# A hybrid attention and mLSTM encoder: 368 weight reloads moved from SP's DMA queue to POOL's

## The chip, the core and the metric

The kernel runs on one core of one Trainium2 chip. A core has a matrix engine (PE, whose weight loads are listed apart as PEld), a vector engine (DVE), a scalar engine (ACT), a general engine (POOL) and SP, which here only issues DMAs. All DMAs are carried out by the same 16 DMA engines. The metric is the device time of one execution in microseconds (us). The kernel before takes 2937.11 us, the median of three runs (2936.93 to 2938.26).

## The reference, cut to what matters

Two sequences (1024 and 2048 tokens of 1024 features, plus 16 learned meta tokens) go through one encoder layer with shared weights:

```python
def _encoder_layer(h, g_pre, w_in, b_in, na_rpb, ml_conv_w, ml_head_g, w_a, w_b, w_out, g_post):
    xn = _rmsnorm(h, g_pre)
    proj = xn @ w_in + b_in                    # 1024 -> 6672 columns
    na_q, na_k, na_v, na_z, ml_qk, ml_v, ml_z, ml_o, ml_g, mg = jnp.split(proj, SPLIT_IDX, axis=-1)
    ya = _neighbourhood_attention(na_q, na_k, na_v, na_rpb)     # 8 x 16 windows on a grid 64 wide
    ya = (ya * jax.nn.silu(na_z)) @ w_a
    yb = (_mlstm_branch(ml_qk, ml_v, ml_g, ml_o, ml_conv_w, ml_head_g) * jax.nn.silu(ml_z)) @ w_b
    ga, gb = jnp.split(jax.nn.sigmoid(mg), 2, axis=-1)
    y = (ga * ya + gb * yb) @ w_out
    return h + _rmsnorm(y, g_post)
```

Everything is 32-bit floating point.

## The kernel before, in words

**Products in two parts.** A 32-bit operand is split into a high part and a rest (`hi`, `lo`), and each product is three matmuls: high by high, high by low, low by high. So every weight tile exists twice, as `whi` and `wlo`, each 128 partitions by up to 1056 words, mostly 512 KB.

**Two streams, one hand-written order on PE.** `run` interleaves a dense stream (the projections and the last products, in the order of `PLAN`) with a sparse stream (`STEPS`: the mLSTM of sequence 0, the attention of sequence 0, the same two for sequence 1). Each generator yields its cost, and the two are advanced in step. PE's order is exactly the order in which the program is written. The order on the other engines and in the DMA queues is set when the program is built, by a scheduler that works from its own estimate of when each instruction could run; within an engine or a queue the order is then fixed, and an instruction that waits holds those behind it.

**Dense stages.** A projection stage (`group`) takes four weight tiles and runs them over two halves of 512 tokens: 24 matmuls a tile and half (`fm_half`, through `mm3`, lines 144 to 146). `tm_unit` (lines 412 to 414) does the columns that are wanted with tokens on the partitions, 24 matmuls of 256 columns for each 128 tokens. A last stage (`final`) for 512 tokens is eight steps of 24 matmuls through `mm3`, one weight pair each, with two gate tiles `tg` read from DRAM per step (line 1267), and then four steps of 4 x 24 matmuls of 256 columns (`prods`, lines 1304 to 1306), two weight pairs each. There are six last stages, and 15 entries in the plan.

**Where the weights come from.** `requests` lists every weight tile in the order of its use. `wload` (line 215) loads a tile from the inputs into `wraw` when it is asked for the first time. `wpump` then makes `whi` (ACT, line 233) and `wlo` (DVE or POOL, line 236) and writes both to DRAM (line 240). When the same tile is asked for again, `wpump` reads the two parts back, lines 230 and 231: two DMAs. There are 184 such reloads, 368 DMAs. `whi` and `wlo` have four buffers each (`NBW`); `wdone`, called when the last matmul on a tile has been written down, frees one and calls `wpump`, so that a reload stands in its queue directly behind the matmuls that free its buffer and waits for them there.

**Queues.** Almost every DMA of the kernel is issued by SP, 2352 of them with the reloads: stores of the projections, loads for the sparse stream, `tg`, the residual input, the output. SP's DMAs report on eight semaphores in turn, and a DMA waits until the one that used its semaphore before, eight places ahead in the queue, has landed. POOL issues 14 DMAs: the one-hot rows `qB` (line 561) and the masks `kx` (line 637) of the attention. Beside them POOL does 82 small memsets (`gt` lines 563 and 564, `g_t` lines 724 and 725, `raw` lines 840 and 842, `va` lines 876 and 877, `st` line 972, `ss` line 287), eight small copies and three of the subtractions of line 236.

**Loads of the sparse stream that the text speaks of:** `qr`, `kr` (`twice`, line 550) at the start of an attention head, `hn`, `tog`, `szg` (line 1170) in the mLSTM's last normalisation, `xh`, `xl` (line 317), the two parts of 512 tokens of the input read back.

Of the kernel before, what the change touches and what calls it, by code (L numbers as in the profile page):

```python
# [9 lines left out]
F32 = mybir.dt.float32  # L10
# [100 lines left out]
class K:  # L111
# [107 lines left out]
    def wpump(self):  # L219


        nc, wp = self.nc, self.wp
        self.wload()
        while self.wraw and self.wout < NBW:
            key, raw, nk, w = self.wraw.popleft()
            n = nk * w
            hi = wp.tile([P, 4 * WU], F32R, name="whi", bufs=NBW)
            lo = wp.tile([P, 4 * WU], F32R, name="wlo", bufs=NBW)
            if raw is None:
                for x, d in zip((hi, lo), self.wkept[key]):  # L230
                    nc.sync.dma_start(x[:, :n].bitcast(F32), d[:, :])
            else:
                nc.scalar.activation(hi[:, :n], raw[:, :n], AF.Copy)
                self.nu += 1
                eng = nc.vector if self.nu > 4 else nc.gpsimd
                eng.tensor_tensor(lo[:, :n], raw[:, :n], hi[:, :n].bitcast(F32), op=ALU.subtract)
                self.wkept[key] = []
                for x, part in ((hi, "h"), (lo, "l")):
                    d = self.dp.tile([P, n], F32, name=f"w{part}{len(self.wkept)}")
                    nc.sync.dma_start(d[:, :], x[:, :n].bitcast(F32))  # L240
                    self.wkept[key].append(d)
            self.wrdy.append([x[:, :n].rearrange("p (k c) -> p k c", k=nk) for x in (hi, lo)])
            self.wout += 1
            self.wload()
# [1248 lines left out]
```

## Time and profile before

| what | us |
|---|---|
| median of three runs | 2937.11 |
| the profiled execution | 2935.2 |
| its span, first to last instruction | 2933.4 |
| PE idle at the start, waiting for `xr` (line 307) | 22.5 |
| PE idle on the other waits of the table of waits, together | 80.3 |
| SP waiting for PE at line 231, the three largest rows | 321.0 |

The span is what the engines' instructions cover; the profiled execution is 1.8 us longer. A row of the profile's table of waits names the instruction that waited, the one that released it, the total, the number of times and the longest. A stretch of the span is described by the busy time of each engine in it, the granted share of PE's clock, the share of time the 16 DMA engines were busy, and the rate in GB/s. In a timeline the columns are start, duration, engine, line, operation, what is written and read, and the number of instructions.

### The profile page before, as it was taken

How to read it: one execution, taken by the hardware profiler on the slowest of the kernel's cores; microseconds unless marked ns; L12 is line 12 of the kernel's file. 1: busy time of each engine (PE TensorE's matmuls, PEld its weight loads, DVE VectorE, ACT ScalarE, POOL GpSimd, SP SyncE). 2: the span in 40 equal slices, each digit the busy share in tenths (PEclk: the TensorE clock that was granted, in tenths of full speed). 3: DMA queues.
4: the chain of work that ended last, by engine and by line, in shares of the span. 5: the costliest groups of instructions: out<-in, count | busy, mean ns of one | idle time of the engine just before them, and what ended most of it. 6: DMA issues, size and time to landing. Idle time of an engine off the chain costs nothing.

```text
span 2933.4 us, 49345 instructions
## 1 busy us (share of the span) xinstructions
PE 2820.8 (96%) x17488; PEld 2510.8 (86%) x17488; DVE 1747.6 (60%) x4722; ACT 1288.7 (44%) x3114; POOL 23.1 (1%) x107
## 2 busy tenths in 40 slices
PE   6999999999799999999999999989999999989998
PEld 6998898899689988888887998977888888879797
DVE  5233566556556665465568776565555557777843
ACT  4213546433344444456566554413444445435421
POOL 1000000000000000000000000000000000000000
PEclk9999999999899999999999999999999999999999
DMA  9655667656775654568679898488568658897875
GB/s 350 219 179 181 197 218 256 232 182 207 255 232 153 198 175 134 168 232 298 197 234 363 277 313 290 136 263 272 172 196 283 191 174 272 245 280 236 283 273 194
DMA packets 438760, 675.25 MB, mean 230 GB/s; under 512 B 52240, under 2 KB 253024, under 8 KB 438512
## 3 DMA queue, kind: packets, MB, share of 16 engines
q1 hardware_dynamic: 437392, 669.41, 70.1%
q0 software_dynamic: 1120, 2.69, 0.4%
q8 instruction: 137, 2.24, 0.3%
q14 instruction: 111, 0.91, 0.1%
HBM read 455.05 MB, written 216.90 MB: 229 GB/s over the span
## 4 chain that ended last, share of the span: by engine, by line
PE 83%; DMA 9%; DVE 5%; ACT 1%; issue 1%; SPq 1%; DVEq 0%; ACTq 0%
PE pj L144 15%; PE pj L145 15%; PE pj L146 15%; PE pj L412 6%; PE pj L413 6%; PE pj L414 6%; PE sm L701 3%; PE pj L1304 3%; PE pj L1306 3%; PE pj L1305 3%; PE tr L689 2%; DMA tg<-gt 2%; PE sc L665 1%; PE sc L664 1%; PE sm L146 1%; PE sm L145 1%
## 5 line engine op out<-in xcount | busy, mean ns | idle before, releaser
L144 PE MATMUL pj<-xh,whi 128*128 128x512 f32 (+1 forms) x1824 | 722.2, 396 | 2.4 <-DVE xl L310 2.2
L145 PE MATMUL pj<-xl,whi 128*128 128x512 f32 (+1 forms) x1824 | 701.3, 384 | 0.6 <-DVE xl L310 0.6
L146 PE MATMUL pj<-xh,wlo 128*128 128x512 f32 (+1 forms) x1824 | 699.8, 384 | 0.0
L412 PE MATMUL pj<-whi,xh 128*128 128x256 f32 (+3 forms) x1576 | 450.8, 286 | 0.0
L413 PE MATMUL pj<-wlo,xh 128*128 128x256 f32 (+3 forms) x1576 | 444.7, 282 | 0.0
L414 PE MATMUL pj<-whi,xl 128*128 128x256 f32 (+3 forms) x1576 | 444.2, 282 | 0.0
L146 PEld LDWEIGHTS pj<-xh,wlo 128*128 128x128 f32 x1824 | 344.6, 189 | 72.3
L144 PEld LDWEIGHTS pj<-xh,whi 128*128 128x128 f32 x1824 | 345.2, 189 | 57.3 <-DVE xl L310 2.6
L145 PEld LDWEIGHTS pj<-xl,whi 128*128 128x128 f32 x1824 | 345.9, 190 | 53.3 <-DVE xl L310 0.8
L412 PEld LDWEIGHTS pj<-whi,xh 128*128 128x128 f32 (+1 forms) x1576 | 294.3, 187 | 1.2
L413 PEld LDWEIGHTS pj<-wlo,xh 128*128 128x128 f32 (+1 forms) x1576 | 294.0, 187 | 1.1
L414 PEld LDWEIGHTS pj<-whi,xl 128*128 128x128 f32 (+1 forms) x1576 | 294.1, 187 | 0.9
L692 DVE TENSOR_TENSOR pts<-tr,pts 96x512 fp32r<-96x512 f32 (+2 forms) x192 | 132.2, 688 | 159.4 <-ACT pts L691 158.3
L672 ACT ACTIVATE prb<-sc,mx 128x384 f32<-128x384 f32 (+2 forms) x192 | 119.4, 622 | 238.2 <-DVE mx L668 234.1
L1304 PE MATMUL pj<-whi,mh 128*128 128x256 f32 x768 | 221.0, 288 | 0.4 <-DMA whi<-wh 0.4
L1306 PE MATMUL pj<-whi,mlo 128*128 128x256 f32 x768 | 217.6, 283 | 2.1 <-DVE mlo L1287 2.1
L1305 PE MATMUL pj<-wlo,mh 128*128 128x256 f32 x768 | 217.2, 283 | 0.0
L691 ACT ACTIVATE pts<-tr 96x512 fp32r<-96x512 f32 (+2 forms) x192 | 114.3, 595 | 170.0 <-PE tr L689 169.3
L421 DVE TENSOR_TENSOR stT<-pj,bb 128x256 f32<-128x256 f32 (+3 forms) x197 | 83.1, 422 | 145.3 <-PE pj L414 141.2
L144 PE MATMUL pj<-yh,whi 128*128 128x512 f32 x384 | 158.0, 412 | 11.0 <-DVE tg L1283 11.0
L668 DVE CUSTOM_DVE_ANT_1 sc<-sc,gt 128x384 f32<-128x384 f32 (+2 forms) x192 | 118.9, 619 | 73.2 <-PE sc L665 67.4
L146 PE MATMUL pj<-yh,wlo 128*128 128x512 f32 x384 | 153.4, 399 | 0.0
(234 smaller groups left out, 5067.5 us busy)
## 6 DMA issues: line engine op xcount, KB each, us to landing
whi<-wh SPq DMA_DIRECT2D x176, 512.0 KB
wlo<-wl SPq DMA_DIRECT2D x176, 512.0 KB
wh<-whi SPq DMA_DIRECT2D x64, 512.0 KB
wl<-wlo SPq DMA_DIRECT2D x64, 512.0 KB
wraw<-w_in SPq DMA_DIRECT2D x48, 512.0 KB
gt<-st SPq DMA_DIRECT2D x96, 256.0 KB
tg<-gt SPq DMA_DIRECT2D x96, 256.0 KB
xh<-xh SPq DMA_DIRECT2D x6, 2048.0 KB
```

The lines of the kernel that those rows point to most:

```text
L144: mm(out, ah, bh, start=start, stop=False)
L145: mm(out, ah, bl, start=False, stop=False)
L146: mm(out, al, bh, start=False, stop=stop)
L412: nc.tensor.matmul(o, xh, wh, start=k == 0, stop=False)
L413: nc.tensor.matmul(o, xh, wl, start=False, stop=False)
L414: nc.tensor.matmul(o, xl, wh, start=False, stop=k == KT - 1)
L668: nc.vector.tensor_tensor_reduce(out=so, in0=so, in1=gt[:, g0:g0 + ns, c0:c0 + 32], op0=ALU.add, op1=ALU.min, scale=-1.0, scalar=3.0e38, a ...
L672: nc.scalar.activation(pr_[:, :N].rearrange("p (b a c) -> p b a c", b=4, c=8), sc[:, :N].rearrange("p (a b c) -> p b a c", b=4, c=8), AF.E ...
L692: nc.vector.tensor_tensor(pts[:ks, :, 1, :], pt[:ks], pts[:ks, :, 0, :].bitcast(F32), op=ALU.subtract)
L1304: nc.tensor.matmul(o, mh[:, k, xs], wh, start=k == 0, stop=False)
L1305: nc.tensor.matmul(o, mh[:, k, xs], wl, start=False, stop=False)
L1306: nc.tensor.matmul(o, ml[:, k, xs], wh, start=False, stop=k == KT - 1)
```

## The change

Both DMAs of a reload are issued by POOL instead of SP. Nothing else in the source is different.

```diff
@@ -228,7 +228,7 @@
             lo = wp.tile([P, 4 * WU], F32R, name="wlo", bufs=NBW)
             if raw is None:
                 for x, d in zip((hi, lo), self.wkept[key]):
-                    nc.sync.dma_start(x[:, :n].bitcast(F32), d[:, :])
+                    nc.gpsimd.dma_start(x[:, :n].bitcast(F32), d[:, :])
             else:
                 nc.scalar.activation(hi[:, :n], raw[:, :n], AF.Copy)
                 self.nu += 1
```

In the built program SP's queue goes from 2352 DMAs to 1984 and POOL's from 14 to 382. PE's order is the same instruction for instruction. The 1984 DMAs that stay on SP keep their order but for small moves: nine in ten move by at most one place, none by more than nine. POOL's DMAs report on eight semaphores of their own in the same way. POOL's memsets and its 14 older DMAs now stand between reloads. DVE's and ACT's orders differ in places from the first reload on.

## The prediction

> **What bounds the kernel now.** I read the page's engine shares first, then its DMA queues, the table of PE's waits, and SP's waits for the queue that the change empties.
>
> ```profile
> PE 2820.8 (96%) x17488; PEld 2510.8 (86%) x17488; DVE 1747.6 (60%) x4722; ACT 1288.7 (44%) x3114; POOL 23.1 (1%) x107
> ...
> q1 hardware_dynamic: 437392, 669.41, 70.1%
> q0 software_dynamic: 1120, 2.69, 0.4%
> ```
>
> PE is the bound, and PE's order doesn't change, so a gain can only come from PE's idle time: 2933.4 - 2820.8 = 112.6 us, of which 22.5 lie at the start, before any reload. POOL is almost unused. The DMA engines are 70% busy on average. The next view shows which loads end PE's waits:
>
> ```profile
> PE tr L1204 <- DVE hn L1193: 15.9, 2, 10.0
> PE sm L701 <- DVE pts L692: 15.7, 12, 4.7
> PE sc L664 <- ACT kd L644: 15.0, 2, 14.1
> PE pj L144 <- DVE tg L1283: 11.0, 5, 5.2
> ...
> PE pj L1304 <- DMA whi<-wh: 0.4, 1, 0.4
> ```
>
> The last line says that reloads are in time: in 184 of them PE waited once, 0.4 us. Three of the other rows are late loads of SP's seen through DVE or ACT (hn, kr and qr, tg). SP's waits:
>
> ```profile
> SPq L231 <- PE pj L146: 203.9, 68, 9.8
> SPq L231 <- PE pj L1306: 86.3, 28, 11.8
> ...
> SPq L231 <- PE pj L414: 30.8, 19, 4.6
> ...
> SPq L550 <- DMA whi<-wh: 13.7, 10, 2.4
> SPq L550 <- DMA wlo<-wl: 13.5, 12, 2.6
> ```
>
> For 321 us SP stands at a reload whose buffer PE has not freed, and other loads are held behind it. The last two rows are a second hold: loads of attention heads wait until a reload, eight places ahead on the same semaphore, has landed.
>
> The longest wait, 780.8 to 794.6 us, in SP's timeline and in two stretches (PE, PEld, DVE, ACT, POOL busy, clock, DMA share, GB/s):
>
> ```profile
> 771.84 0.53 SPq L317 DMA_DIRECT2D xh<-xh  x1
> 772.46 0.73 SPq L317 DMA_DIRECT2D xl<-xl  x1
> 773.29 2.56 SPq L231 DMA_DIRECT2D whi<-wh  x1
> 775.95 2.84 SPq L231 DMA_DIRECT2D wlo<-wl  x1
> 778.88 1.20 SPq L348 DMA_DIRECT2D mk<-st  x1
> 780.13 1.26 SPq L550 DMA_DIRECT2D qr<-nq  x1
> ```
>
> ```profile
> 765.00:780.00 15.00, 15.00 (x75) 12.41 (x74) 6.50 (x18) 7.23 (x13) 0.00 (x0) 1.00 1.02 373
> 780.00:795.00 15.00, 0.89 (x4) 0.34 (x2) 4.14 (x5) 2.10 (x3) 0.00 (x0) 0.62 0.94 290
> ```
>
> PE has nothing to do because `qr` comes late; but the DMA engines are full, so issuing it earlier gains only what bytes ahead of it allow.
>
> **The change, part by part.** *What leaves SP*: 368 issues, at the median of 0.37 us (line 231's rows) 138 us of SP's time, and the waits above. Three places where a freed SP reaches a late load sooner:
>
> (a) Start of the first attention. In the built order `qr` now follows `xl` and one `xr`, and the `mk` store comes after the head's loads. SP reaches `qr` up to 2.56 + 2.84 + 1.20 = 6.6 us sooner. Bytes still count: `xh` and `xl` (2.1 MB each) and the reloads (1.05 MB) are 5.2 MB, at 373 GB/s 14.1 us from 771.8, so 785.9; the four loads of `qr` and `kr` (0.62 MB) take it to 787.6; from the last landing to PE's start are 2.4 us today (792.1 to 794.6). So 790.0 instead of 794.6: -4.6. Bounds 0 and -6.6.
>
> (b) The mLSTM's last normalisation, where PE waits 10.0 us near 1943. In the 40 us around it SP waits 2.3 and 1.5 us for landings of `wlo` and `whi` ahead of the `hn` loads. Those go: -3.8. Bounds 0 and, if the reload pair's bytes ahead also go (1.05 MB at the 299 GB/s of 1925 to 1945, 3.5 us), -7.3.
>
> (c) The last stages: 11.0 us on `tg` in 5 waits. A `tg` behind a reload pair waits for 1.31 MB; when the two rings take turns packet by packet, 4 KB against 2 KB, it waits for three times its own 0.26 MB, 0.79 MB: 0.52 MB less, 1.3 us at the 390 GB/s of 2840 to 2865. Of the five waits (5.3, 2.9, 2.1 and two of some 0.6 us) three lose 1.3 and two vanish: -4.9. Bounds 0 and, with the pair's 1.05 MB gone altogether (2.7 us each), -8.6.
>
> Together -13.3. The 15.7 us on `pts` are a chain of DVE and ACT, no load; the other rows have none above 4 us: 0.
>
> *What POOL gets.* A DMA on POOL shows 0.51 us each (line 637). 368 of twice the rows cost 188 to 376 us of an engine that is 1% busy: nothing, as long as it is in time. Landing after issue is 3.1 / 7.2 / 9.0 us (least, median, most) for `kx`, 192 to 256 KB. A reload is about twice that; each DMA engine moves eight 4 KB packets of it, at 0.16 us (median in the trace), where `kx` of 208 KB makes four: 0.6 us more, 7.8 at the median. The deadlines: in the last steps of a last stage two pairs are in use and two on their way, and 96 matmuls at 0.12 us spacing give 11.5 us. Matching every reload in the trace with the first matmul that reads its tile, issue to use is 7.2 us at the least, 9.8 for one in a hundred, 12.6 for one in twenty, 21.4 at the median. So 7.8 is covered for all but one or two: 0. At 9.6 (9.0 + 0.6) four of 368 are late by up to 2.4: bounds 0 and +10. If both halves come one after the other, that is a rival below.
>
> *What is queued behind POOL's new waits.* The reloads wait for PE, and POOL's own work behind them with it. Two places count. `qB`, `gt` and `kx` of the first attention ran at 628 to 687; in the new order they stand behind a reload that SP got off at 773.3 and 776.0, so `kx` goes out by 779 and lands 5.9 to 7.7 us later (medians of the page's DMA groups), at 787 at the latest: under the 790.0 of (a), cover 3 us; gone, (a) is lost, no more. `va`, `raw` and `st` before the second mLSTM ran at 1184; they come behind the reload that SP issued at 1208.0, and their reader on ACT started at 1214.6, when `raw` landed: 5 us of cover. Both 0. The second attention's `kx` are ready some 20 us before their use.
>
> *DMA time.* The page's queue lines give 0.004 x 16 x 2933 us over 2.69 MB, 70 ns a KB, on POOL's queue and 49 on SP's; but POOL's DMAs so far fill only half the partitions. Packet against packet (medians over the trace) it is 98 against 84 ns at 2 KB. I take those 14 ns more for each: 47,000 packets, 16 engines, 41 us of DMA time, hidden where the engines are 60 to 70% busy. In 1540 to 1790 and 2460 to 2933 they are 91 and 80% busy; 150 reload DMAs fall there, 17 us. Taken: +3. Bounds 0 and +17.
>
> *DVE.* No row shows what a POOL DMA does to a DVE instruction beside it. If each meeting costs the 0.51 us of the issue, and issues fill 368 x 0.51 / 2933, some 6% of the time, then line 681's 192 scalings meet 12 of them, 6 us on DVE; in a chain that PE waits on in 12 places: +1, bounds 0 and +10.
>
> The Trainium skill (SBUF — State Buffer, section "Who interferes with whom") says that descriptors for POOL's DMAs are written through a port pair that DVE's two-port operations lock, so that such DMAs stall behind DVE. The `kx` rows fit it without proving it: 7.2 us for 0.2 MB, and 3.1 at the least. By that rule the outcome would be the third rival's, priced there from rows.
>
> Sum: -13.3 + 3 + 1 = -9.3. The profiled execution took 2935.2 (its span 2933.4 and 1.8 around it), so 2925.9; it lies 1.9 under the median, so 2928. With all bounds on one side: 2937 - 6.6 - 7.3 - 8.6 = 2914.5, and 2937 + 10 + 17 + 10 = 2974.
>
> **The rivals.**
>
> 1. *Only the order of service changes.* In every stretch with a late load the DMA engines are 90 to 100% busy (0.94 and 1.02 above); a byte moved forward pushes another back. Against it: in (b) SP stood idle on a semaphore. Then 2937, give or take 4. For it the DMA share, against it SP's 321 us of waits. The Trainium skill (DMA: Bandwidth & Descriptors, section "Issuing engines are not separate DMA queues") says just this: DMAs of all issuing engines interleave on the same 16 DMA engines, and issuing from more of them saves only sequencer time. The trace before has too few POOL DMAs to show it.
>
> 2. *The reloads take turns with loads that stood ahead of them* (the other side). Today a small load ahead of a reload in SP's queue pays nothing for it. With two rings each of its packets, 0.5 to 2 KB, waits for one of 4 KB: 16 packets of a pair, 0.16 us each, 2.5 us. There are about ten load-bound stalls (two hn, two kd, five tg, one yr): +25, less the 8 of what SP no longer waits for: 2954. It decides where the late load was issued before the reload; at 717 to 722 (the `tog` loads of the first normalisation) it was, at 2627 and 781 it wasn't.
>
> 3. *POOL's reloads come late.* If the two halves land one after the other at 9 us each, 18 us against 11.5 of lead: 6.5 us in each of 24 steps, +156, 3093. Against it the 3.1 us that a POOL DMA also took. A milder form, half of the steps and 3 us, gives 2973.
>
> **How the numbers follow.** What a measurement here can tell from no change is about 0.2%, 5.9 us. The forecast has 0.50 (its own range 2914 to 2936: 0.40 faster, 0.10 same), the first rival 0.12 (0.02, 0.08, 0.02), the second 0.28 and the third 0.10 (both slower). Faster 0.42, same 0.18, slower 0.40. The range runs from 6 below the forecast's lower bound, for waits that I count at 0, over the second rival with 6 to spare; it leaves out the third, and some 0.1 beside it: 2908 to 2960.
>
> **What would show it.** Right: SP's rows at line 231 gone, the waits on `kd` and `hn` of PE shorter by about 5 and 4 us, no wait of PE on `whi` or `wlo` above a few us. Wrong: rows of PE on DMA `whi` or `wlo` (third rival), or `tg`, `hn`, `pts` rows longer with SP's own waits gone (second).

## The result, and the profile after

The changed kernel takes 2943.9 us, the median of 12 runs (2937.07 to 2948.21); the kernel before, run beside it, 2935.9 (12 runs, 2924.82 to 2938.26). The ratio is 1.0035, with a 95% interval from 1.0025 to 1.0046: 0.35% slower. The profiled execution after has a span of 2946.4 us, before 2933.4: 13.0 us more. It was the longest of its twelve (2948.21 us), so a good part of these 13.0 us is scatter: the medians are 8.0 us apart.

The page after, engine shares and DMA queues (queue: packets, MB, share of 16 engines):

```profile
PE 2823.3 (96%) x17488; PEld 2513.0 (85%) x17488; DVE 1747.1 (59%) x4722; ACT 1288.8 (44%) x3114; POOL 217.7 (7%) x475
...
q1 hardware_dynamic: 384400, 476.18, 50.3%
q0 software_dynamic: 54112, 195.91, 19.8%
```

POOL took over 368 issues for 195 us of its time. Together the two queues fill 70.1% of the DMA engines, before 70.5%: in total the packets on POOL's queue took no more of the engines' time than on SP's. DVE's busy time is the same to 0.5 us, PE's to 2.5. What grew is PE's idle time, 112.6 to 123.1 us.

The reloads are in time. First their row in the page's DMA issues (KB each, us to landing), then the last line of an answer on line 231 alone:

```profile
whi<-wh POOLq DMA_DIRECT2D x176, 512.0 KB, 6.3
```

```profile
DMA to landing us min/median/max: 3.6/6.3/12.3
```

PE's table of waits after has no row for `whi` or `wlo`. Its largest load-bound rows:

```profile
PE sc L664 <- DVE stk L642: 22.5, 1, 22.5
...
PE tr L1204 <- DVE hn L1193: 18.3, 2, 9.9
PE sm L701 <- DVE pts L692: 8.4, 6, 3.7
PE pj L144 <- DVE tg L1283: 7.4, 5, 2.6
...
PE pj L307 <- DVE xl L310: 5.3, 5, 2.3
```

`tg` and `pts` wait less than before (11.0 and 15.7), but the start of attention waits 22.5 us instead of 14.1, the norm 18.3 instead of 15.9 and `xl` 5.3 instead of 3.1.

SP did not become free. Its largest rows after:

```profile
SPq L356 <- ACT st L341: 144.6, 47, 7.2
SPq L606 <- DVE mx L668: 103.1, 30, 10.8
SPq L356 <- ACT yg L705: 83.1, 17, 7.5
SPq L1377 <- DVE yo L1376: 82.5, 16, 50.0
```

Rows 1 and 3 were 77.4 and 52.6. All rows of SP's table added up make 1867 us before and 2012 after: the queue is still in order, and now stands at stores whose data ACT or DVE has not made yet, where it stood at reloads.

**Where the time went.** PE's order is the same in both, so matmul can be set against matmul. How much later the same matmul starts, after against before, grows in three steps by 1000 us; after that it goes on to 20.9 at 2600 in smaller steps (+3.44 at 1667 the largest) and falls back:

| matmul that waits | before | after | step, us |
|---|---|---|---|
| L1204, first norm of the mLSTM | 735.6 | 739.2 | +4.05 |
| L307, transposes of the next input | 768.8 | 775.0 | +2.49 |
| L664, first score of the attention | 794.6 | 809.2 | +8.35 |
| L144, with `tg`, near 2638 | 2638.2 | 2652.2 | -5.42 |

At 1000 us the lag is 10.7 us (smaller steps give some back), at 2000 us 17.0, at the end 12.9. The text follows the three steps before 1000 us; what lies behind was not taken apart.

*Step 1.* DVE after, then before, near 730 us (start, duration, engine, line, operation, idle time and releaser):

```profile
732.79 0.69 DVE L1178 SCALAR_TENSOR_TENSOR hn<-tog,hn 128x512 f32<-128x512 f32 x1 [3.86 <-DMA tog<-to]
...
736.05 2.13 DVE L1192 TENSOR_SCALAR hn<-hn,mv,nwy 128x128 f32<-128x128 f32 x8
...
738.26 1.28 DVE L1193 TENSOR_TENSOR hn<-hn,szg 128x512 f32<-128x512 f32 x2
```

```profile
732.34 2.13 DVE L1192 TENSOR_SCALAR hn<-hn,mv,nwy 128x128 f32<-128x128 f32 x8
...
734.54 1.28 DVE L1193 TENSOR_TENSOR hn<-hn,szg 128x512 f32<-128x512 f32 x2
...
736.16 0.68 DVE L1178 SCALAR_TENSOR_TENSOR hn<-tog,hn 128x512 f32<-128x512 f32 x1
```

The same product with `tog` (L1178, for the next block) stands behind the norm before, and ahead of it after. In DVE's fixed order the norm then waits for a load that it does not need. That `tog` was issued 5.1 us earlier than before (721.6 for 726.7), but landed only 1.3 us earlier (732.8 for 734.1): four reloads issued on POOL beside it, between 721.1 and 723.0, landed from 728.4 to 734.0.

*Step 2.* ACT after, near 770 us:

```profile
768.60 0.61 ACT L309 ACTIVATE xh<-pj 128x512 fp32r<-128x512 f32 x1
772.55 1.06 ACT L290 ACTIVATE xsq<-xr 128x1024 bf16<-128x1024 f32 x1 [3.34 <-DMA xr<-x_sample]
...
773.61 1.06 ACT L309 ACTIVATE xh<-pj 128x512 fp32r<-128x512 f32 x2
```

The square of the second `xr` (L290) was behind these `xh` before; now they wait 3.34 us with it for its load.

*Step 3.* SP after, then ACT and DVE after, at the start of attention:

```profile
777.06 0.53 SPq L317 DMA_DIRECT2D xh<-xh  x1
777.69 0.62 SPq L317 DMA_DIRECT2D xl<-xl  x1
778.40 3.51 SPq L282 DMA_DIRECT2D xr<-x_sample  x1
781.96 3.94 SPq L550 DMA_DIRECT2D qr<-nq  x2
```

```profile
799.90 1.06 ACT L290 ACTIVATE xsq<-xr 128x1024 bf16<-128x1024 f32 x1 [15.20 <-DMA xr<-x_sample]
...
800.95 0.61 ACT L639 ACTIVATE stk<-qr 128x512 fp32r<-128x512 f32 x1
```

```profile
803.46 4.87 DVE L296 SCALAR_TENSOR_TENSOR xr<-xr,nwy,gain 128x1024 f32<-128x1024 f32 x4
808.37 0.69 DVE L642 TENSOR_TENSOR stk<-qr,stk 64x512 fp32r<-64x512 f32 x1
```

The fourth `xr` load went six places back, behind 4 MB of stores, and landed at 799.8 (before 774.5). In both kernels its square on ACT and its four products on DVE (4.87 us) stand ahead of the head's `stk`; before they were done by then, now the head waits for them. The load, in the prediction's words "one `xr`", was the one that counted most. The head's own loads were late as well: the second `qr` landed at 800.7 (before 792.1) and the last `kr` at 802.7 (before 793.5), 9.2 us later where PE was already 6.3 us behind. So some 3 us of the step are these loads, and the rest is the work on `xr` in front of `stk`. The stretches, against those of the prediction (PE, PEld, DVE, ACT, POOL busy, clock, DMA share, GB/s):

```profile
765.00:780.00 15.00, 11.82 (x64) 9.57 (x63) 4.05 (x6) 8.52 (x16) 2.30 (x5) 1.00 0.81 274
780.00:795.00 15.00, 6.74 (x30) 5.13 (x28) 0.00 (x0) 0.69 (x1) 3.34 (x10) 0.87 1.05 371
795.00:810.00 15.00, 0.66 (x1) 0.29 (x1) 8.45 (x19) 4.29 (x7) 0.00 (x0) 0.50 0.87 270
```

Over these 45 us the DMA engines are nearly as full as before (0.91 on average, before 0.94); the hole in PE has moved from 780 to 795 and grown.

### The profile page after: what moved, and what is told of

Its sections match the earlier page's. It is cut to its first block, busy times and chain, and to the rows that moved or that the text cites. A ratio compares the mean times of both kernels' runs of the same rounds, so it can differ in the third digit from the quotient of the medians.

```text
span 2946.4 us, 49350 instructions
## 1 busy us (share of the span) xinstructions
PE 2823.3 (96%) x17488; PEld 2513.0 (85%) x17488; DVE 1747.1 (59%) x4722; ACT 1288.8 (44%) x3114; POOL 217.7 (7%) x475
## 4 chain that ended last, share of the span: by engine, by line
PE 59%; DMA 7%; DVE 4%; ACT 1%; issue 1%; SPq 0%; DVEq 0%; ACTq 0%
PE pj L144 11%; PE pj L145 11%; PE pj L146 11%; PE sm L701 3%; PE pj L1306 3%; PE pj L1304 3%; PE pj L1305 3%; PE tr L689 3%; PE pj L412 2%; PE pj L413 2%; PE pj L414 2%; DMA tg<-gt 2%; DMA um<-ud 2%; PE sc L665 1%; PE sc L664 1%
## 5 line engine op out<-in xcount | busy, mean ns | idle before, releaser
L144 PE MATMUL pj<-xh,whi 128*128 128x512 f32 (+1 forms) x1824 | 721.7, 396 | 0.9 <-ACT st L343 0.9
L144 PEld LDWEIGHTS pj<-xh,whi 128*128 128x128 f32 x1824 | 345.1, 189 | 55.6 <-ACT st L343 1.1
L231 POOL DMA_DIRECT2D whi<-wh x184 | 98.0, 533 | 1130.1 <-PE pj L146 1115.4
L144 PE MATMUL pj<-yh,whi 128*128 128x512 f32 x384 | 157.7, 411 | 7.4 <-DVE tg L1283 7.4
L668 DVE CUSTOM_DVE_ANT_1 sc<-sc,gt 128x384 f32<-128x384 f32 (+2 forms) x192 | 119.0, 620 | 71.8 <-PE sc L665 70.5
```

The source lines that it names most:

```text
L144: mm(out, ah, bh, start=start, stop=False)
L668: nc.vector.tensor_tensor_reduce(out=so, in0=so, in1=gt[:, g0:g0 + ns, c0:c0 + 32], op0=ALU.add, op1=ALU.min, scale=-1.0, scalar=3.0e38, a ...
```

## The experiments

Two theories. *Order*: the scheduler, given another set of DMAs in SP's queue, set instructions of DVE, ACT and SP in another order, and that costs the time. *Queues* (or *taking turns*, the prediction's second rival): reloads in a second queue share the DMA engines with loads that stood ahead of them. They are told apart by holding an order and changing the queue alone. All runs below that hold an order do so with edges that order two instructions of one engine without a wait (shortened here and below; in `pin`, words stand for the lists of instructions):

```diff
+def pin(tc, chains):                     # one list for each engine held
+    traced = list(tc.nc.cur_bb.bb.instructions)
+    for order in chains:
+        for a, b in zip(order, order[1:]):
+            tc.add_manual_dep(traced[b], traced[a].name, NoSync, reason="order")
```

Each run's ratio is against the kernel before on the same chip; "lag" is how much later the same matmul starts than in the first profile of the kernel before.

**How far a profile repeats.** The kernel before with its own order held, the same program:

> The kernel before, its own order on SP, ACT, DVE and POOL written out as edges: the same instructions in the same order, run once more to see how far one matmul moves between two profiled executions of one program. 2925 to 2939 us; the first L664 starts within 2 us of 794.6 us and no single matmul shifts by more than 2 us. A larger shift would say that the jumps read from single profiles so far are partly noise.

2938.67 us, one run. The first L664 moved by 1.11 us; the largest steps were 2.27, 2.01 and 1.53, two of them a little more than expected. The span came out 3.5 us longer than in the first profile. So a step of 3 us at a named place can be read, and the end of a single profile is good to about 4 us; for the whole, the ratios count. Step 2 (+2.49) lies under that mark and counts because it comes back in two kernels below with the same order there (+3.99 and +2.35) and in none that has ACT's old order.

**Order and queue crossed.** All reloads on POOL in the order of before:

```diff
+    pin(tc, [SP of before without reloads, ACT of before, DVE of before])
```

> All reloads on POOL, as in the changed kernel, but SP (without its reloads), ACT and DVE held to the order of the kernel before. Theory 'order': the loss came from the order that the scheduler chose once the reloads had left SP; the queue itself gave the gain of the last stages (about -9 in the traces between 2600 and 2650). Then 2924 to 2931 us, the wait of the first `sc` L664 back from 22.5 to 14 us or less, and no late norm near 739. Theory 'queues': reloads on a second queue take turns with the loads of the attention head and of the norm, whatever the order. Then 2940 to 2947 us, the first L664 still waits 20 us or more and the lag of about 4 us near 739 stays.

1.0033, interval 1.0022 to 1.0044. Neither theory whole: the three steps are gone, or smaller (lag -0.8 at 750 and at 780, +3.82 at L664), and the lag at 1000 us is -0.1 instead of 10.7; but the last stages lose, and it ends at +8.8.

Reloads on SP in the order of after:

```diff
-                    nc.gpsimd.dma_start(x[:, :n].bitcast(F32), d[:, :])
+                    nc.sync.dma_start(x[:, :n].bitcast(F32), d[:, :])
+    pin(tc, [SP of after, ACT of after, DVE of after, POOL of after without reloads])
```

> The other corner: reloads on SP, as in the kernel before, but SP (without its reloads), ACT, DVE and POOL held to the order of the changed kernel. 'Order': the loss comes without POOL's queue too: 2940 to 2955 us, first `sc` L664 waits 20 us or more. 'Queues': 2933 to 2939 us, first L664 waits about 14 us.

1.0076, interval 1.0055 to 1.0097. As "order" has it, the loss comes without POOL's queue: +5.27 at 735.6, +3.99 at 768.8. L664's wait of 13.3 us was not the 20 foretold, so that step needs the queue or something else; the places of the reloads in SP's queue were left to the scheduler here. The median, 2956.6 us, lies above both ranges, and the loss is more than twice that of the change; the profiled execution (2948.3) was the second fastest of six, so its trace does not show where the rest went, and that stays open.

**One load put back.**

```diff
 SP of after: mk L348, xr L282 (third),
+xr L282 (fourth),
 yb L1208 x4, xh L317, xl L317,
-xr L282 (fourth),
 qr L550 x2, kr L550 x4
```

> The changed kernel in its own order, with one instruction moved: SP issues the fourth `xr` load (L282) six places earlier, ahead of the `yb` stores and of the `xh` and `xl` stores (L317), where the kernel before had it. 'Order': the +8.35 us at the start of attention came from this one load, which stood behind 4 MB of stores and held `xsq`, the rsqrt and `xr` on ACT and DVE ahead of the head's chain. The first L664 waits 14 us or less and the kernel takes 2934 to 2938 us. 'Queues': the load is late because reloads share the engines with it; the first L664 still waits 20 us or more and the time stays within 2941 to 2947 us.

1.0026, interval 1.0014 to 1.0038. The step at L664 fell from +8.35 to +2.35, the lag at 1000 us to 7.7; the wait itself is still 16.5 us, not 14, and the time did not come down as far as "order" said. Its interval meets that of the changed kernel, so here it is the step that shows the effect, not the time.

**Three places put back.** With the one above, the other two steps:

```diff
 DVE of after:
-hn L1178, bs L1180 x4 (next block)
 nwt L133 ... hn L1192 x8, hn L1193 x2,
+hn L1178, bs L1180 x4 (next block)
 ACT of after:
-xsq L290 (second xr)
 xh L309 x2, ybo L1205, xh L309
+xsq L290 (second xr)
```

> The changed kernel in its own order, with three places put back: DVE's first `hn` L1178 of the block near 730 us (with its four `bs` L1180) behind the norm that it had been set ahead of; ACT's `xsq` L290 of the second `xr` behind the `xh` L309 that it had been set ahead of; SP's fourth `xr` load (L282) ahead of the `yb` and `xh` stores. If these three readers and loads, set elsewhere by the scheduler, are the loss: the lag at 1000 us falls from 10.7 to 1 to 4 us and the kernel takes 0 to 0.2% more than the kernel before. If the loss is spread over the rest of the order (some 80 other instructions of these engines stand elsewhere before 1100 us) or is the queue's: 0.25% or more.

1.0004, interval 0.9991 to 1.0017, which does not meet the interval of the changed kernel. The lag at 1000 us is 2.1. Its waits of PE:

```profile
PE sc L664 <- ACT kd L644: 17.5, 2, 17.1
...
PE tr L1204 <- DMA nv<-stT: 6.7, 1, 6.7
PE tr L1204 <- DVE hn L1193: 6.3, 1, 6.3
...
PE pj L144 <- DVE tg L1283: 5.9, 4, 2.4
```

The two waits of L1204 are 13.0 us together, in the changed kernel 18.3 and before 15.9. Seven instructions of 9310 on these three engines (SP without reloads) account for the loss, as far as this interval tells; with them back, and the rest of the order of after, the change costs nothing and brings nothing. Why the scheduler set them elsewhere wasn't looked into.

**The order of before up to 1100 us, that of after from there.**

```diff
+    pin(tc, [before up to 1100 us + after from there, for SP, ACT, DVE])
```

> The changed kernel (all reloads on POOL), with the order of the kernel before on SP, ACT and DVE up to 1100 us and that of the changed kernel from there. If the changed kernel's loss before 1100 us is its order (lag 10.7 us there, against 1 to 3 with the order of before), and the losses of the other kernel in the last stages are of its order with POOL's queue, then this one has neither: 2933 to 2939 us, 0 to 0.2% over the kernel before. If the loss is the queue's in any order: 0.3% or more.

1.0004, interval 0.9991 to 1.0016: the same from the other side. The loss lies in the order before 1100 us. It also says that the last-stage loss of the kernel with all reloads on POOL in before's order belongs to that order together with POOL's queue, and that the changed kernel doesn't have it.

**Which reloads.** In the order of before, on POOL only those of the last stages (shown), and only those of the projections (`key[0] == "i"` in the same place):

```diff
-                    nc.gpsimd.dma_start(x[:, :n].bitcast(F32), d[:, :])
+                    (nc.gpsimd if key[0] in "mo" else nc.sync).dma_start(x[:, :n].bitcast(F32), d[:, :])
```

> Only the reloads of the last stages (weights w_a, w_b and w_out, 160 of the 368 transfers) on POOL; those of the projections stay on SP, and SP, ACT and DVE keep the order of the kernel before. Both theories: the waits of `tg` (L1283) give back what they did in the changed kernel, 2925 to 2931 us. They differ in what it has over the kernel with all reloads on POOL in the same order: 'order' says within 4 us of it, 'queues' says 8 us or more ahead of it.

> The complement: only the projections' reloads (208 of 368 transfers) on POOL, those of the last stages on SP, order of the kernel before. 'Taking turns': the start of attention is 2 to 5 us late as with all reloads on POOL, about half of which the DVE and DMA work behind it gives back; the last stages are those of the kernel before; 2931 to 2938 us, 0 to 0.2% over the kernel before. 'Order alone': within 0.1% of the kernel before and no delay at the start of attention.

Last stages alone 1.0026 (1.0010 to 1.0041), projections alone 0.9997 (0.9985 to 1.0008). The second is as "taking turns" has it, with L664 later by 4.81; the first missed what both said of its time (2938.3 us against 2925 to 2931), and lies 3.2 us ahead of the kernel with all reloads on POOL in the same order, within the 4 us that "order" gave. In that order the loss is in the last stages.

**Taking turns, by itself.** Before's order and queue, but two weights (four transfers) ahead of the attention on POOL:

```diff
+                    (nc.gpsimd if self.nrel // 2 in (21, 22) else nc.sync).dma_start(x[:, :n].bitcast(F32), d[:, :]); self.nrel += 1
```

> The kernel before in its own order, all reloads on SP but for two weights (four transfers of 512 KB) ahead of the attention's start, which go out of POOL's queue. 'Taking turns': these four go out some 4 and 15 us earlier, share the DMA engines with the `xh` and `xl` stores of 2 MB each, whose transfers take 14 to 21 us rather than 8.7 and 13.0, and the head's loads behind them land 2 to 4 us later: the first L664 starts 2.5 to 5 us later than in the kernel before. 'Order alone': with the order held nothing moves, L664 starts within 1 us of the kernel before.

2934.84 us, one run. L664 starts 3.29 us later. The four reloads went out 3 to 5 and 14 us earlier and landed 9 to 12 us earlier; the stores `xh` and `xl` beside them took 16.0 and 20.1 us (before 8.7 and 13.0), and the head's loads landed 3 us later. SP's timeline and a stretch of this run:

```profile
772.66 0.78 SPq L317 DMA_DIRECT2D xl<-xl  x1
773.63 2.56 SPq L348 DMA_DIRECT2D mk<-st  x1
776.24 10.91 SPq L550 DMA_DIRECT2D qr<-nq  x2
787.20 1.09 SPq L550 DMA_DIRECT2D kr<-nk  x1
```

```profile
780.00:795.00 15.00, 0.50 (x3) 0.07 (x1) 3.27 (x3) 0.00 (x0) 0.00 (x0) 0.64 1.04 379
```

The engines are full (1.04, before 0.94), so what the reloads gained the stores and the head lost. This is one profile, but the same step is +3.50 to +4.81 in four other kernels with these reloads on POOL and before's order at this place, and +0.85 to +1.89 in three with them on SP. The 3.3 us were given back soon: the lag at 850 us is 0.1.

**Does one queue for `tg` and reloads help?** All reloads on POOL in the order of before, and `tg` on POOL too:

```diff
-                    nc.sync.dma_start(tg, self.GT[s][8 * br + ft][:, t0:t0 + n])
+                    nc.gpsimd.dma_start(tg, self.GT[s][8 * br + ft][:, t0:t0 + n])
```

> All reloads on POOL in the order of the kernel before, and the gate loads `tg` (L1267) with them in POOL's queue. 'Taking turns': the last stages lost because `tg` on SP, behind other loads, shared the engines with reloads issued later than it; in one queue it is served before them again, and the kernel takes 5 to 10 us less than with `tg` on SP: within 0.15% of the kernel before. 'POOL as such' (its issues, or transfers that are slower from it): no better than with `tg` on SP, 0.3% or more over the kernel before. A third way: `tg` stands behind reloads that wait for PE, and the kernel is over 0.5% slower.

1.0027, interval 1.0015 to 1.0038, between what the first two ways said. PE's wait on `tg` fell from 9.4 to 3.1 us and the time did not follow: late `tg` is not the whole of that order's last-stage loss. What it is stays open.

**The opposite change.** Reloads on SP as before, `tg` alone on POOL; then the loads of all attention heads as well; then, of these, only the first head of each of the two calls. All in the order of before:

```diff
-                    nc.sync.dma_start(tg, self.GT[s][8 * br + ft][:, t0:t0 + n])
+                    nc.gpsimd.dma_start(tg, self.GT[s][8 * br + ft][:, t0:t0 + n])
...
+        eng = nc.gpsimd if j == 0 else nc.sync        # in na_prep: qr, kr, vr, zt
```

> The opposite of the change, in the order of the kernel before: the reloads stay on SP and the gate loads `tg` (L1267, 96 transfers of 256 KB), which matmuls of the last stages wait for, go out of POOL's queue. 'Taking turns': what has a queue of its own is served ahead of what stands in the common one, so `tg` lands in 4 us or less in the median (before 5.1), the waits of L1283 behind them nearly go, and the kernel takes 5 to 12 us less than the kernel before. 'Order alone': the queue of a transfer does not matter, the time stays within 4 us of the kernel before.

> As the run with `tg` on POOL, and the loads of the attention heads too (L550, L629, L630, L633, 456 transfers with `tg`). 'Taking turns': the first L664 starts 5 us or more earlier than in the kernel before, since its loads no longer stand behind the `xh` and `xl` stores, and the kernel takes 10 to 20 us less. 'Order alone': within 4 us of the kernel before. A third way: POOL's in-order queue makes a load wait for the buffer of the load ahead of it, and the kernel takes 10 us or more longer.

> `tg` on POOL and reloads on SP, and of the heads' loads only those of the first head of each of the two attention calls (18 transfers) on POOL. 'Taking turns': the first L664 starts 5 to 8 us earlier than in the kernel before, as it did with all heads on POOL, and the second head, on SP as before, loses less than the 10 us it lost there: 2918 to 2926 us, 0.2 to 0.5% under the kernel before. Rival: the engines are full from 770 to 800 us, what the first head gains the second loses: as with `tg` alone, 2925 to 2931 us.

`tg` alone: 2927.9 us, 0.9984 (0.9972 to 0.9995), and its waits are nearly gone:

```profile
PE pj L144 <- DVE tg L1283: 1.9, 2, 1.5
```

Not for the reason given: `tg` landed no faster (5.5 us in the median, before 5.1); it was issued earlier, 9.5 us ahead of its use in the median instead of 7.9. All heads: 1.0021 (1.0010 to 1.0033), outside all three ranges; the first L664 starts 7.50 us earlier and the second loses 10.45. The second head's own loads are not what it waits for: they went out on POOL from 788.7 and all but `vr` landed by 799.7. What came late is a load of the first head that stayed on SP:

```profile
805.02 0.57 DVE L668 CUSTOM_DVE_ANT_1 sc<-sc,gt 128x384 f32<-128x384 f32 x1 [14.48 <-DMA gt<-rpb]
```

SP issued this `gt` at 786.9, and it landed at 804.9, behind loads that POOL issued after it. With the second head's loads left on SP, in the next kernel, the same `gt` went out at 787.6 and landed at 797.7. That is taking turns once more. `tg` with only the first heads: 2925.0 us, 0.9976 (0.9965 to 0.9987), faster than both kernels, though the interval meets that of `tg` alone. L664 starts 8.24 us earlier, at 788.0; the second head loses 3.40. On POOL the first head's `qr` went out at 697.9 instead of 781.4: its buffer was free all that time, and only the place in SP's queue held it. What PE waits for there now is `stk` (lines of this kernel are one higher there):

```profile
PE sc L665 <- DVE stk L643: 5.9, 1, 5.9
```

## Why the prediction was wrong

It said 2928 and faster. The sign is wrong; the range (2908 to 2960) holds the result only because it was drawn over the second rival's 2954, not by the forecast's mechanism.

**The step that failed** is (a), -4.6 between 0 and -6.6: "In the built order `qr` now follows `xl` and one `xr`". The step here was +8.35. It counted SP's issue times and the bytes ahead of `qr`, and did not ask who reads that `xr` and what stands behind the reader on ACT and DVE. (It also took 792.1 us for the last landing; that is the second `qr`, and the last `kr` landed at 793.5, 1.1 us and not 2.4 before PE's start.) The same omission left out two steps altogether: the text on the change says that "DVE's and ACT's orders differ in places", and the sum has no term for it; they cost +4.05 and +2.49. With the three places put back the time is that of the kernel before. With them back (a) is still wrong, +2.95 and not -4.6, because the reloads take turns with what is ahead of `qr`, as the two weights alone showed with +3.29.

**(b)**, -3.8 near 1943: right in kind. The step was -1.60 in the changed kernel, -3.30 with three places put back. That it is the work of the reloads' queue is not shown: the repeated profile has no step there (+0.07), but with `tg` alone moved and all reloads still on SP it was -3.07, with only four transfers moved -1.48, and with all reloads on SP in the order of after -1.28. What it needs stays open.

**(c)**, -4.9 on `tg`: the row fell from 11.0 to 7.4 us, and to 5.9 with the places put back, so -3.6 and -5.1; the repeated profile has 9.9. Its mechanism, a `tg` that lands sooner by its share in turns, does not show in the median: `tg` landed 5.8 us after the end of its issue, before 5.1, and was issued 8.9 us ahead of its use instead of 7.9. Near 2638, where the row lost most, the late `tg` did land in 6.3 us instead of 10.0, but it also went out 7.8 us earlier against PE's matmuls, which alone covers the step of -5.42. In the kernels that move `tg` itself the row fell by issuing earlier, too.

**Nothing for the reloads' landing**: right. 6.3 us at the median against the 7.8 worked out, no wait of PE. **Nothing for what is queued behind POOL's waits**: the 0 came out, its working did not. `kx` went out at 781.4 and 782.0, not by 779, and landed at 793.2, not at 787; that cost nothing only because `kr` landed later still, at 802.7. **DMA time, +3** (0 to +17): 0; packets of 4 KB on POOL's queue filled no more of the engines than on SP's. **DVE, +1**: 0, busy 1747.1 against 1747.6 us. The third rival, with it the rule that it drew on from the Trainium skill (SBUF — State Buffer, "Who interferes with whom"), didn't come about: the slowest reload took 12.3 us, PE did not wait for one, and no issue on POOL took more than 0.73 us. Whether DVE ran its two-port operations beside them is not in these traces.

**The first rival**, 2937 because "a byte moved forward pushes another back", had 0.12. It is what the change does once the order is repaired: 1.0004. For it stood the DMA share; against it the 321 us for which SP waited at reloads, but that time was not won: SP's waits went up by 146 us, at stores. The rule beside it in the Trainium skill (DMA: Bandwidth & Descriptors, "Issuing engines are not separate DMA queues"), that DMAs of all engines interleave on the same 16, agrees with the two weights alone (`xh` 16.0 us for 8.7). Its second half, that issuing from several engines saves only the sequencer's time, is too narrow here: a second queue let `qr` go out 83 us earlier (697.9 for 781.4), past what stood ahead of it in order.

**The second rival** had its mechanism right and its places wrong. It was to decide at 717 to 722, but the two `tog` issued there took 5.0 and 6.9 us to land, before 6.6 and 6.5. The next one took 11.1 us instead of 7.4, but was issued 5.1 us earlier and landed earlier all the same; the loss there needed DVE's order, and came with that order also when the reloads were on SP (+5.27). And the rival was excluded at 781, where it cost 3 us.

## What to carry to other kernels

In this kernel a second queue was worth having for transfers whose buffer was free and whose reader was waiting, not for those that wait for a buffer: moving 368 reloads with slack brought nothing (and in the whole order of before cost 0.33%, for a reason that stays open), moving 114 wanted loads gained 0.24%. When a scheduler sets the order, a change of queue can change every engine's order, as it did here: compare the orders of both programs, look for a reader of a load that now stands ahead of work that doesn't need it, and put that back before judging the change. And where the DMA engines are full (1.04 in the stretch with the two weights), an earlier issue is paid by another transfer: ask whose bytes it delays.

## What the runs showed of the hardware

Behind two stores of 2 MB with POOL's reloads beside them, SP took 10.91 us to issue two `qr` loads of 128 KB each, 9.73 of them for the first, and SP's table of waits has no row for that line in this stretch; before, with the reloads on SP, two took 2.67 us. It came again with three places put back (9.77 us for the first) and with one load put back (8.28). The cause wasn't tried.

A reload on POOL lands 5.8 us after the end of its issue in the median, on SP 5.1 (`whi`, 184 each, issues matched with landings in the traces), and its issue takes 0.53 us of POOL against 0.37 of SP. Transfers on POOL's queue can land ahead of ones that SP issued before them: `xh` took 16.0 us instead of 8.7 beside two weights, and `gt` landed at 804.9 though `qr` and `kr`, issued 1.7 us and more after it, were there by 799.7.
